# Token-block staging of x, PLE blocks of 272, a w_out block held back and early roots in a hybrid decoder layer

## The chip, the cores and the metric

The kernel runs on the 8 cores of one Trainium2 chip (two dies: cores 0 to 3 and 4 to 7). Each core computes its own share of the batch. The metric is the device time of the slowest core, in microseconds (us). In a slow run one die shows a clearly lower granted TensorE clock than usual. Comparisons use fast runs alone. A median quoted as the time of a kernel is over all its runs, slow ones included; where that matters, the mean of the fast runs is given.

PE is TensorE, PEld its weight loads, DVE is VectorE, ACT is ScalarE, POOL is GpSimd, SP is SyncE.

## The reference, cut to what matters

One layer: a half-step SwiGLU FFN, a mixer (pooling and gated linear attention), one output projection, a second half-step FFN, a gated per-layer embedding (PLE), and a final norm.

```python
h = x + 0.5 * swiglu(rmsnorm(x, ffn1_norm), ...)          # FFN 1, 1024 -> 2816 -> 1024
z = rmsnorm(h, mix_norm) @ w_in                            # mixer: 4 heads
...
mix = sigmoid(ga) * a_out + sigmoid(gb) * (rmsnorm(o) * silu(g))
h = h + mix @ w_out                                        # w_out products
h = h + 0.5 * swiglu(rmsnorm(h, ffn2_norm), ...)           # FFN 2
gate = sigmoid(rmsnorm(h, ple_norm) @ w_ple_gate)          # PLE
h = h + gate * (p @ w_ple_proj)
y = rmsnorm(h, final_norm)
```

A core has 1088 tokens in its first half and 1024 in its last half; it does the whole layer for the first half and then for the last. Values lie feature-major: 128 partitions, 8 groups of features (KC), tokens along the free axis.

## The kernel before

The program is a list of operations that a scheduler (a list scheduler with a cost model) puts in order at build time. Every engine then works through its own list in that order. So an operation that is placed badly holds up those behind it. The parts that the change touches:

```python
FBLK = (tuple((272 * i, 272) for i in range(4)), BLK[1])            # FFN blocks of tokens
PBLK = (BLK[0], ((0, 512), (512, 256), (768, 256)))                 # PLE blocks: 320, 384, 384 in the first half
RESERVE = 3                                                         # PSUM banks kept free for the oldest operation
...
def load_x(self, sb, first):          # x goes straight into the residual h, through hardware queues
    for bi, (st, sz) in enumerate(FBLK[sb]):
        for q in range(0, KC, n):
            self.dma(h[:, q:q + n, st:st + sz], self.xT[sb][:, q:q + n, st:st + sz], ...)
...
# first half, FFN 1: the first weights wait until x has come far enough
self.load_x(sb, first)
self.load_gu(1, 0, after=self.hk(sb, b0[0], b0[1], 1))
self.load_gu(1, 1, after=self.hk(sb, b0[0], b0[1], 7))
prev = []
for bi, (st, sz) in enumerate(FBLK[sb]):
    for k in range(KC):
        self.square(sb, k, st, sz, 'act' if k % 2 == 0 else 'dve', after=prev)
    r = self.norm_rstd(sb, st, sz, 'd')
    prev = K(r)                                        # squares of the next block wait for this root
    self.norm_apply(sb, V_FFN1, st, sz, r)
...
# gate/up: the first 3 of 22 steps are plain products; from step 3 on, 7 products with sums of
# weights (wT, wguh, made by VectorE) and sums of x (sx) replace 8
# mixer, last head: a block's tail, then its own 64 w_out matmuls and the norm of FFN 2
def cur():
    middle(it)
    tail(it)              # ... if hd == 3: w_out of this block
...
# PLE of the first half: all roots and outputs after it, two output buffers
y = [fw.tile("yt%d" % i, [128, 4, W], F32, b1(4 * W * 4)) for i in range(2)]
def finals():
    for bi in range(3):
        root(bi)
    for bi in range(3):
        final(bi)
```

A *root* is the reciprocal square root of a norm on ScalarE: logarithm and exponential, from one table set. The activations of PLE and FFN (tanh, silu) come from another set. A change of set is one table load (1.28 us in these traces).

## Time and profile before

The median is 1588.53 us (runs of 1587.28 to 1588.62 us, one slow one of 1643.35). The profiled run is disturbed on die 1 (granted clock 0.971 to 0.978, against 0.985 on die 0). So stage times of the kernel before are read on cores 0 to 3, and the windows below are of core 0. The spans of die 0 are 1574.9 to 1583.8 us.

From the page of the profile (slowest core): the busy times, then the chain of waits, that is, the work that ended last followed backwards, as shares of the span.

```profile
span 1600.1 us, 29026 instructions; the slowest of 8 cores (1574.9 to 1600.1 us)
...
PE 1503.3 (94%) x9808; PEld 930.3 (58%) x9808; DVE 956.4 (60%) x1898; ACT 758.1 (47%) x1533; POOL 242.4 (15%) x424
...
PE 82%; DVE 7%; DMA 5%; issue 3%; ACT 3%; POOL 0%; DVEq 0%; ACTq 0%; POOLq 0%; SPq 0%
```

PE is the bound. It idles for 1600.1 - 1503.3 = 97 us, and it is mainly these that can be won. Where they lie, the windows view of core 0 says. Its columns: the stretch, its length, the busy time and instructions of each engine, the granted clock (PEclk), the busy share of the DMA engines, and the rate.

```profile
core 0: us, PE busy (x) PEld busy (x) DVE busy (x) ACT busy (x) POOL busy (x), PEclk, DMA share, GB/s
0.00:20.00 20.00, 3.06 (x14) 1.79 (x15) 8.65 (x21) 5.20 (x12) 3.54 (x10) 1.00 0.85 211
20.00:40.00 20.00, 17.98 (x136) 13.28 (x134) 16.00 (x41) 14.13 (x26) 0.00 (x0) 1.00 0.65 134
40.00:60.00 20.00, 18.97 (x161) 15.24 (x159) 14.59 (x40) 7.77 (x20) 4.22 (x8) 1.00 0.71 96
...
510.00:520.00 10.00, 9.54 (x64) 5.74 (x62) 7.38 (x14) 6.37 (x11) 0.00 (x0) 1.00 0.70 182
520.00:530.00 10.00, 10.00 (x69) 6.20 (x67) 4.48 (x9) 4.98 (x10) 0.00 (x0) 1.00 0.26 100
...
870.00:880.00 10.00, 5.56 (x18) 2.04 (x19) 6.29 (x13) 1.79 (x3) 0.53 (x1) 0.66 1.03 252
...
1280.00:1290.00 10.00, 7.53 (x36) 3.28 (x35) 6.03 (x8) 5.39 (x8) 0.00 (x0) 1.00 0.04 13
1290.00:1300.00 10.00, 10.00 (x48) 4.55 (x47) 4.15 (x6) 3.52 (x6) 0.00 (x0) 1.00 0.00 0
1300.00:1310.00 10.00, 4.67 (x21) 1.62 (x18) 4.11 (x7) 5.31 (x7) 0.00 (x0) 1.00 0.00 0
1310.00:1320.00 10.00, 8.79 (x26) 3.10 (x27) 6.96 (x12) 1.12 (x2) 1.14 (x3) 0.66 0.26 38
...
1560.00:1570.00 10.00, 0.38 (x2) 0.13 (x2) 6.09 (x10) 4.18 (x9) 0.00 (x0) 0.69 0.24 90
1570.00:1580.00 10.00, 0.00 (x0) 0.00 (x0) 5.64 (x15) 0.00 (x0) 0.00 (x0) 0.50 0.95 330
```

There are four gaps: the start; 870 us, after the first half's PLE; 1300 to 1320 us, the end of the second mixer; and the last 20 us. At 1310 PE counts as 8.79 of 10 us busy, but it did 26 matmuls where a full stretch has 48: after the idle before, the granted clock was 0.66. The Trainium skill ("TensorE: Matmul & The Clock Gate", "Part 1: The HAM clock gate") says that an idle window of about 3.4 us puts PE's clock to half until it has been busy again. The 0.66 here, a mean over 10 us, agrees with the half: the clock record in the trace has 6.8 us of half clock from 1311.1 us on. But the longest single idle time in the 6.8 us before that was 3.1 us (more in the last section).

What ends the wait at 870 us, from the waits view (engine, line, what it writes, what it waited for: us in total, times, longest), VectorE's line and TensorE's:

```profile
DVE yt L445 <- DMA yT<-yt: 9.5, 2, 6.6
...
PE ps L483 <- DVE snap L450: 7.7, 3, 6.3
```

VectorE waits for a store to leave an output buffer (yt), and PE waits behind VectorE.

### The profile page before, as it was taken

The page shows a single profiled execution, that of the slowest core. Times are in us where ns is not written, and L with a number is a line of the kernel's source. Part 1 is how long each engine was busy: PE and PEld are TensorE (multiplying, and loading weights), DVE is VectorE, ACT ScalarE, POOL GpSimd, SP SyncE. Part 2 cuts the span into 40 slices and gives each one's busy share as a digit, 9 for nine tenths or more (in the row PEclk, how much of TensorE's full clock was granted, in tenths as well). Part 3 has the DMA queues.
Part 4 walks back from the last instruction along what each step waited for, and adds up shares of the span by engine and source line. Part 5 has one row for each costly group of instructions (what it writes and reads, how often), then busy time and mean ns, then how long its engine had stood idle before and what let it go on. Part 6 is the DMA issues. An engine that isn't in the chain of part 4 may idle for free.

```text
span 1600.1 us, 29026 instructions; the slowest of 8 cores (1574.9 to 1600.1 us)
## 1 busy us (share of the span) xinstructions
PE 1503.3 (94%) x9808; PEld 930.3 (58%) x9808; DVE 956.4 (60%) x1898; ACT 758.1 (47%) x1533; POOL 242.4 (15%) x424
## 2 busy tenths in 40 slices
PE   5999999999989999999998899999999988999994
PEld 3788887666656678888753344445555533444444
DVE  6766436677878577743566665236666656664435
ACT  4455314566566456641253344125667543442144
POOL 0221000112100011112061121001021001121113
PEclk9999999999999999999999899999999998999997
DMA  7777642769833355439309875413386004684503
GB/s 173 96 115 122 117 74 47 170 126 185 183 79 80 106 74 86 70 66 151 60 1 209 179 117 100 74 37 49 66 133 99 1 4 73 85 146 80 92 1 106
DMA packets 81633, 153.30 MB, mean 96 GB/s; under 512 B 9520, under 2 KB 23120, under 8 KB 81488
## 3 DMA queue, kind: packets, MB, share of 16 engines
q0 software_dynamic: 53760, 110.22, 43.7%
q1 hardware_dynamic: 27040, 40.64, 8.4%
q8 instruction: 82, 1.34, 0.3%
q10 hardware_dynamic: 688, 0.58, 0.1%
q14 instruction: 63, 0.52, 0.1%
HBM read 243.00 MB, written 18.61 MB: 163 GB/s over the span
## 4 chain that ended last, share of the span: by engine, by line
PE 82%; DVE 7%; DMA 5%; issue 3%; ACT 3%; POOL 0%; DVEq 0%; ACTq 0%; POOLq 0%; SPq 0%
PE ps L483 79%; DVE xn L445 3%; DMA wgu<-w1u 2%; DMA yT<-yt 2%; DVE snap L450 1%; DVE yt L445 1%; ACT nrs L440 1%; DMA wd<-w2d 1%; PE ps L1221 1%; DMA h<-xT 0%; ACT L367 0%; PE ps L1297 0%; PE ps L1299 0%; DMA wgu<-w2u 0%; PE ps L1304 0%
## 5 line engine op out<-in xcount | busy, mean ns | idle before, releaser
L440 ACT ACTIVATE snap<-ps 128x272 f32<-128x272 f32 (+1 forms) x492 | 226.2, 464 | 181.6 <-PE ps L483 163.3
L483 PE MATMUL ps<-xn,wfm 128*128 128x384 bf16 (+2 forms) x1600 | 310.7, 345 | 1.0 <-ACT nrs L440 0.4
L483 PE MATMUL ps<-xn,wgu 128*128 128x272 bf16 (+1 forms) x1488 | 271.8, 319 | 13.5 <-DVE xn L445 12.0
L483 PE MATMUL ps<-hid,wd 128*128 128x272 bf16 (+1 forms) x1892 | 270.3, 305 | 3.1 <-DVE hid L450 2.2
L483 PEld LDWEIGHTS ps<-hid,wd 128*128 128x128 bf16 x1892 | 184.9, 98 | 86.2 <-issue 4.3
L483 PEld LDWEIGHTS ps<-xn,wfm 128*128 128x128 bf16 x1600 | 152.8, 99 | 123.9 <-issue 10.5
L440 ACT ACTIVATE xn<-h 128x272 bf16<-128x272 f32 (+3 forms) x152 | 75.4, 504 | 292.6 <-DVE h L445 284.9
L483 PEld LDWEIGHTS ps<-xn,wgu 128*128 128x128 bf16 x1488 | 146.0, 99 | 100.8 <-issue 34.6
L445 DVE SCALAR_TENSOR_TENSOR h<-ps,h 128x272 f32<-128x272 f32 (+3 forms) x136 | 74.0, 546 | 185.9 <-PE ps L483 185.7
L483 PE MATMUL ps<-sx,wT 128*128 128x272 f16 (+1 forms) x912 | 173.9, 322 | 2.0 <-DVE wT L450 1.4
L450 DVE TENSOR_TENSOR hid<-snap 128x272 bf16<-128x272 f32 (+1 forms) x228 | 118.4, 520 | 65.8 <-ACT snap L440 63.0
L450 DVE TENSOR_TENSOR snap<-ps,snap 128x272 f32<-128x272 f32 (+1 forms) x228 | 114.1, 520 | 44.6 <-PE ps L483 29.5
L483 PEld LDWEIGHTS ps<-sx,wT 128*128 128x128 f16 x912 | 90.8, 100 | 54.9 <-issue 17.3
L483 PE MATMUL ps<-xn,wT 128*128 128x272 bf16 (+1 forms) x456 | 90.1, 321 | 17.8 <-DVE snap L450 17.5
L440 ACT ACTIVATE ps<-ps 128x272 f32<-128x272 f32 (+1 forms) x114 | 51.3, 450 | 114.5 <-PE ps L483 109.7
L445 DVE SCALAR_TENSOR_TENSOR xn<-h,vecs,nrs 128x272 bf16<-128x272 f32 (+3 forms) x168 | 85.2, 581 | 30.2 <-ACT nrs L440 30.1
L367 ACT ACT_TABLE_LOAD x77 | 98.8, 1283 | 4.0 <-issue 2.6
L460 POOL DMA_DIRECT2D wfm<-win_fm x80 | 42.5, 532 | 311.6 <-PE ps L483 131.9
L483 PE MATMUL ps<-xnh,wguh 128*128 128x272 f16 (+1 forms) x456 | 88.2, 317 | 0.1
L483 PE MATMUL ps<-sx,wgu 128*128 128x272 f16 (+1 forms) x456 | 87.9, 316 | 0.0
L460 POOL DMA_DIRECT2D wgu<-w2g x44 | 23.3, 530 | 365.9 <-PE ps L483 311.7
L483 PEld LDWEIGHTS ps<-xn,wT 128*128 128x128 f16 x456 | 43.4, 99 | 48.5 <-issue 31.8
(150 smaller groups left out, 1889.3 us busy)
## 6 DMA issues: line engine op xcount, KB each, us to landing
wfm<-win_fm POOLq DMA_DIRECT2D x80, 256.0 KB, 6.2
wgu<-w1g POOLq DMA_DIRECT2D x44, 256.0 KB, 5.3
wgu<-w1u POOLq DMA_DIRECT2D x44, 256.0 KB, 6.4
wd<-w1d POOLq DMA_DIRECT2D x16, 704.0 KB, 7.0
wgu<-w2g POOLq DMA_DIRECT2D x44, 256.0 KB, 4.2
wgu<-w2u POOLq DMA_DIRECT2D x44, 256.0 KB, 5.2
S0t<-sgla SPq DMA_DIRECT2D x32, 256.0 KB, 6.3
ngs<-S0t SPq DMA_DIRECT2D x32, 256.0 KB, 5.9
```

The lines of the kernel that those rows point to most:

```text
L367: eng.preload_act_table_set(TABLES[tbl])
L440: self.fw.add('act', lambda e: e.activation(out=R(out), in_=R(in_), func=func, **kw), reads, writes, cost=0.19 + n / 1200.0, tbl=tbl)
L445: self.fw.add('dve', lambda e: e.scalar_tensor_tensor(out=R(out), in0=R(in0), scalar=scalar, in1=R(in1), op0=op0, op1=op1), reads, writes, ...
L450: self.fw.add('dve', lambda e: e.tensor_tensor(out=R(out), in0=R(in0), in1=R(in1), op=op), reads, writes, cost=0.16 + n / 960.0)
L460: self.fw.add('pool', lambda e: e.dma_start(out=dst, in_=src), reads=after, writes=[key], dma=sem, cost=nbytes / 330e3)
L483: ins = e.matmul(R(out), lhsT=l, rhs=r, start=(start and i == 0), stop=(stop and i == n - 1), skip_group_check=skip)
L1221: ins = e.matmul(R(pS[:, q * 256:(q + 1) * 256]), lhsT=km[:, q, :], rhs=vS[:, :], start=True, stop=True)
```

## The change

The intent: start PE earlier, and fill or remove the gaps. x and y lie in token blocks in memory. x of the first half is staged in the weights' own queue, interleaved with the first weights, and loaded into h a second time later. PLE of the first half goes in four blocks of 272, with two of the norms and the outputs inside it and four output buffers. In the last head of the mixer, the w_out products of the last but one block are held back beside the last block's tail. Roots are scheduled with priority. The PSUM reservation goes from 3 to 2.

```diff
-PBLK = (BLK[0], ((0, 512), (512, 256), (768, 256)))
+PBLK = (FBLK[0], ((0, 512), (512, 256), (768, 256)))
-    RESERVE = 3
+    RESERVE = 2
@@ scheduler
-                    if best is None or t < best[0]:
-                        best = (t, i, e)
+                    if best is None or t - op['bonus'] < best[0]:
+                        best = (t - op['bonus'], i, e, t)
@@ start of the first half
+        x(0, 4)                 # staging tiles xs, in the weights' queue
+        self.load_gu(1, 0)
+        x(1, 4)
+        self.load_gu(1, 1)
+        x(2, 4)
+        x(3, 4)
+        self.load_gu(1, 2)
...
                 for k in range(KC):
-                    self.square(sb, k, st, sz, 'act' if k % 2 == 0 else 'dve', after=prev)
+                    self.square(sb, k, st, sz, 'act' if (k % 2 == 0 if bi == 0 else k % 4) else 'dve', src=xs)
@@ both halves: x into h from gate/up step 8 on
+        for n, (bi, q) in enumerate((b, q) for b in range(len(FBLK[sb])) for q in (0, 4)):
+            at.setdefault(8 + n, []).append(lambda bi=bi, q=q, n=n: self.load_h(sb, bi, q, 8 + n))
@@ PLE (the roots in both halves, the blocks in the first)
-                self.act(rf[bi][:, 0:sz], ps[:, 0:sz], AF.Copy, [pk], K(rf[bi]))
+                fw.bonus = 2.0
+                self.rsqrt(rf[bi], ps, sz, pk)
+                fw.bonus = 0.0
...
-            for bi in range(3):
+            for bi in range(4):
                 for c in range(KC):
                     ple(bi, c)
+                    if bi < 2:
+                        self.norm_apply(sb, V_PLE, st, sz, rn[bi + 2], ks=(c,))
+                if bi:
+                    final(bi - 1)
-            self.finals = finals
+            self.finals = lambda: final(3)
@@ PLE, last half
-            if c >= 2:
-                ple(0, c - 2)
+            if c >= 4:
+                ple(0, c - 4)
@@ mixer, last head (outp: the w_out products and the norm of a block)
+                if it['hd'] == 3 and it['bi'] < nbk - 2:
+                    outp(it)
...
             else:
-                cur()
+                middle(it)
+                fw.merged([lambda: tail(it), lambda: outp(items[i - 1])])
+                outp(it)
... (cut: layouts of the inputs and outputs, buffers)
```

## The prediction

> **What bounds it now.** TensorE: in the first part of the page PE is busy 1503 of 1600 us (94%), and the chain of waits is 82% PE. So only PE's 97 idle us can be won; the change removes no sizeable matmul. The windows view of the slowest core (7, granted clock 0.974) says where PE idles: 0:60 us 19.8; 60:510 13; 510:570 (end of the first mixer) 7.3; 784:860 (PLE of the first half) 4.9; 860:900 (start of the second half's FFN) 11; 1280:1330 (end of the second mixer) 9.3; 1575:1600 21.
>
> **Step by step.**
>
> 1. Start: gain 1.5 us. Now the first weights are asked for at 11.8, the first weight matmul runs at 20.6, and x's last block arrives at 32.6. In one queue x0, gate/up 0, x1 ... arrive one after the other (Trainium skill, "DMA: Bandwidth & Descriptors", "Queues, rings and completion order": an engine consumes a ring in order, and takes turns between queues). First weight matmul near 12. But the emitted order puts ScalarE's squares of blocks 2 and 3 before the root of block 1, so PE has only block 0 until the last x lands; 4.45 MB of x plus weights at some 300 GB/s (the hardware queue's bytes over its share of busy time) puts that near 26. Ten groups of 16 matmuls (1.84 us each) remain, so the first combined-weight product moves only from 50.3 to 48.5.
>
> 2. x is loaded again into h (4.45 MB while DMA is 75% busy, 100:160). Weights are fetched two steps (17 us) ahead: cost 0.5 us.
>
> 3. End of the mixers: w_out of the previous block (64 matmuls, 10.6 us, second half 13.8) fills the last tail (osq to mix, 9 to 13 us), and the next FFN's first matmuls fill the last norm (now waits of 2.6 and 3.1 us on VectorE's xn). Gain 5 + 7 us.
>
> 4. PLE in four blocks of 272, norms and outputs inside. Now the output products come late, at 843-881, with two yt buffers: VectorE waits 8.8 us for a yT store, and PE behind it 8.3 us (waits view), while reloads of h and weights fill the DMA (share 1.05). Four buffers, early roots and later loads of h remove that. Price: per block about 10 us each of PE, VectorE (8x0.44 + norm 3.3 + output 3.4) and ScalarE (two more table loads of 1.28), so small new stalls. Idle of 784:975 falls from 18 to 8: gain 10 us.
>
> 5. The end: now all roots and outputs wait until 1582, and VectorE works through 24 products until 1595.5. With early roots only eight (3.3 us) remain after the last root: end 4 us of store after 1585. Gain 9.5 us.
>
> Sum 32 us: **1556 us**, 8 in 10 between 1541 and 1571. Faster by over 2%: 0.52, within 2%: 0.46, slower: 0.02.
>
> **What would show it.** PE idle near 65 us with PE busy unchanged; about 10 us after the last matmul, not 20; no PE wait over 4 us near 860-885, none over 2 us at either mixer's end; the first weight matmul near 12, yet the first combined-weight product not before 46.
>
> **What would make it wrong.** x slower than 300 GB/s in the one queue; VectorE, slowed by GpSimd's adds beside it (512-wide xn took up to 1.49 instead of 0.74 us in PLE), or ScalarE's table loads starving PE in PLE; a lower clock on die 1 (0.81-0.93 at 880:950 already); the PSUM reservation going from 3 to 2 reshuffling the steady stages.

## The result, and the profile after

The changed kernel takes 1566.34 us (median of 4 runs: 1562.7, 1563.75 and 1568.93 us, and a slow one of 1645.31). The ratio to the kernel before is 0.9855, 95% interval 0.9821 to 0.989: 1.45% faster, within 2%. The means of the fast runs are 1588.1 us before and 1565.1 us after. Ratios are the mean time of one kernel's fast runs over that of the other's of the same rounds, so not quite the ratio of the medians quoted. The profiled run is fast, with a granted clock of 0.990 to 0.994 on all cores.

```profile
span 1562.2 us, 29356 instructions; the slowest of 8 cores (1552.6 to 1562.2 us)
...
PE 1483.3 (95%) x9896; PEld 933.8 (60%) x9896; DVE 955.6 (61%) x1908; ACT 769.4 (49%) x1559; POOL 253.1 (16%) x440
...
PE 81%; DMA 7%; DVE 5%; issue 3%; ACT 3%; POOL 1%; DVEq 0%; ACTq 0%; POOLq 0%
```

PE's idle time fell from 97 to 1562.2 - 1483.3 = 79 us; 65 had been predicted. PE's busy time fell by 20 us as well. That is not less work: the page before is of a core on the slower die. Between undisturbed cores (the mean of cores 0 to 3 before, of all eight after) idle time fell from 92.9 to 74.7 us and busy time from 1486.4 to 1482.7 us.

Stage by stage, read from the first matmul (or VectorE output) of each stage in the traces. Before is the mean of cores 0 to 3, after the mean of all eight.

| stage | before, us | after, us | change | predicted |
|---|---|---|---|---|
| start to the 9th output of the combined products (the first of gate/up step 5) | 67.2 | 70.7 | +3.5 | -1.5 |
| from there to the first down matmul | 108.9 | 111.3 | +2.4 | +0.5 |
| down | 84.0 | 84.0 | 0 | 0 |
| first mixer, to the next gate/up's first combined product | 313.3 | 312.5 | -0.8 | -5 |
| FFN 2, first half | 207.9 | 209.1 | +1.2 | 0 |
| PLE, first outputs, next gate/up | 198.1 | 190.8 | -7.3 | -10 |
| down | 79.2 | 79.2 | 0 | 0 |
| second mixer, to the next gate/up's first combined product | 264.4 | 251.3 | -13.1 | -7 |
| gate/up, last FFN | 117.1 | 116.5 | -0.6 | 0 |
| last down and PLE, to the last matmul | 119.1 | 124.0 | +4.9 | -9.5 for this row and the next |
| last matmul to the end | 20.3 | 8.0 | -12.3 | |
| sum | 1579.5 | 1557.4 | -22.1 | -32.5 |

The sum of -22.1 us is about what the timed runs show as well (23.0 us between the means of the fast runs). (The terms as written make -32.5; the prediction called it 32.)

The windows of core 0, where before had its gaps:

```profile
core 0: us, PE busy (x) PEld busy (x) DVE busy (x) ACT busy (x) POOL busy (x), PEclk, DMA share, GB/s
0.00:20.00 20.00, 5.00 (x20) 2.29 (x21) 7.95 (x19) 6.30 (x15) 7.78 (x18) 1.00 0.84 184
20.00:40.00 20.00, 15.00 (x104) 11.05 (x103) 10.24 (x25) 14.24 (x28) 0.00 (x0) 0.83 0.49 136
40.00:60.00 20.00, 16.65 (x140) 13.67 (x138) 14.87 (x41) 5.53 (x14) 3.17 (x6) 0.97 0.61 79
...
510.00:520.00 10.00, 7.32 (x52) 4.21 (x52) 6.73 (x14) 4.31 (x8) 0.00 (x0) 1.00 0.82 175
520.00:530.00 10.00, 7.85 (x54) 4.84 (x55) 6.41 (x12) 6.67 (x14) 0.00 (x0) 1.00 0.51 182
...
870.00:880.00 10.00, 10.00 (x48) 4.49 (x46) 6.02 (x13) 4.45 (x8) 1.95 (x4) 1.00 0.59 82
...
1300.00:1310.00 10.00, 10.00 (x48) 4.57 (x47) 8.05 (x13) 1.79 (x3) 2.11 (x4) 1.00 0.44 58
1310.00:1320.00 10.00, 10.00 (x48) 4.50 (x46) 7.38 (x16) 4.15 (x7) 2.11 (x4) 1.00 0.79 114
...
1540.00:1550.00 10.00, 8.96 (x81) 7.61 (x79) 6.59 (x16) 7.39 (x16) 5.16 (x8) 0.99 0.38 154
1550.00:1560.00 10.00, 1.25 (x8) 0.39 (x6) 5.89 (x14) 4.60 (x10) 1.70 (x2) 0.69 0.30 119
```

The gaps at 870 and at 1300 are gone, and the one behind the last matmul is down from 20.3 to 8.0 us. But a new one is at 510 to 530 us, and the start is worse: PE begins earlier (5.00 against 3.06 us before 20 us) and then does 104 matmuls where it did 136.

Why, the timeline of ScalarE on core 0 shows (start, duration, what it does, and the idle time before with what ended it):

```profile
23.52 1.06 ACT L442 ACTIVATE xn<-xs 128x272 bf16<-128x272 f32 x3
25.04 1.07 ACT L442 ACTIVATE xn<-xs 128x272 bf16<-128x272 f32 x3 [0.46 <-DMA xs<-xT]
26.50 1.07 ACT L442 ACTIVATE xn<-xs 128x272 bf16<-128x272 f32 x3 [0.40 <-DMA xs<-xT]
28.83 1.07 ACT L442 ACTIVATE xn<-xs 128x272 bf16<-128x272 f32 x3 [1.26 <-DMA xs<-xT]
29.91 1.28 ACT L369 ACT_TABLE_LOAD   x1
31.21 0.69 ACT L442 ACTIVATE nrs<-ps 128x272 f32<-128x272 f32 x2
```

The squares of blocks 2 and 3 (xn<-xs) stand before the roots of blocks 1 and 2 (nrs<-ps, x2), and three of the four groups wait for their piece of x. So block 1, which had landed at 18.6 us, gets its root at 31.2 us. The blocks were all issued in one queue between 1.6 and 9.1 us and were waited for one after the other until 28.8 us. The Trainium skill ("DMA: Bandwidth & Descriptors", "Queues, rings and completion order") says that each DMA engine consumes the descriptors of a ring in order, which the prediction used; it does not promise that they finish in that order, but here the waits came in the order of issue. And a second time an engine's order costs: the timeline of VectorE a little later, where it makes the weight sums of steps 3 and 4:

```profile
53.22 0.42 DVE L452 TENSOR_TENSOR wT<-wgu,wT 128x512 f16<-128x512 bf16 x1
57.73 0.43 DVE L452 TENSOR_TENSOR wT<-wgu 128x512 f16<-128x512 bf16 x1 [4.10 <-DMA wgu<-w1u]
58.08 0.42 DVE L452 TENSOR_TENSOR wguh<-wgu 128x512 f16<-128x512 bf16 x1
```

The second line is the first sum of step 4, which waits 4.1 us for weights; the third belongs to step 3, whose weights are there (its own first sum ran at 51.25), and stands behind it. PE waits 3.3 us for that wguh.

### The profile page after: what moved, and what is told of

It is laid out like the page before. It is cut to its first block, busy times and chain, and to the rows that moved or that the text cites. A ratio compares the mean times of both kernels' runs of the same rounds, so it can differ in the third digit from the quotient of the medians.

```text
span 1562.2 us, 29356 instructions; the slowest of 8 cores (1552.6 to 1562.2 us)
## 1 busy us (share of the span) xinstructions
PE 1483.3 (95%) x9896; PEld 933.8 (60%) x9896; DVE 955.6 (61%) x1908; ACT 769.4 (49%) x1559; POOL 253.1 (16%) x440
## 4 chain that ended last, share of the span: by engine, by line
PE 81%; DMA 7%; DVE 5%; issue 3%; ACT 3%; POOL 1%; DVEq 0%; ACTq 0%; POOLq 0%
PE ps L485 79%; DMA wgu<-w1u 4%; DMA xs<-xT 1%; DVE snap L452 1%; ACT L369 1%; DMA wgu<-w2u 1%; DVE xn L447 1%; DMA wd<-w2d 1%; POOL h L469 1%; PE ps L1234 1%; DVE yt L447 0%; PE ps L1310 0%; DVE fsg L447 0%; PE ps L1317 0%; ACT nrs L442 0%
## 5 line engine op out<-in xcount | busy, mean ns | idle before, releaser
L485 PE MATMUL ps<-xn,wgu 128*128 128x272 bf16 (+1 forms) x1488 | 266.3, 316 | 7.4 <-DVE xn L447 7.4
L442 ACT ACTIVATE xn<-h 128x272 bf16<-128x272 f32 (+3 forms) x136 | 69.4, 513 | 279.9 <-DVE h L447 279.8
L485 PE MATMUL ps<-sx,wT 128*128 128x272 f16 (+1 forms) x912 | 166.9, 312 | 0.9 <-ACT ps L442 0.9
L369 ACT ACT_TABLE_LOAD x85 | 109.1, 1283 | 2.5 <-PEq L431 1.1
L485 PE MATMUL ps<-xn,wT 128*128 128x272 bf16 (+1 forms) x456 | 86.9, 313 | 12.3 <-DVE snap L452 12.0
L485 PE MATMUL ps<-xn,wpg 128*128 128x272 bf16 (+2 forms) x448 | 66.7, 291 | 9.9 <-ACT fsg L442 9.2
L447 DVE SCALAR_TENSOR_TENSOR xn<-h,vecs,nrs 128x272 bf16<-128x272 f32 (+3 forms) x120 | 65.2, 614 | 16.1 <-ACT nrs L442 15.9
```

The source lines that it names most:

```text
L369: eng.preload_act_table_set(TABLES[tbl])
L442: self.fw.add('act', lambda e: e.activation(out=R(out), in_=R(in_), func=func, **kw), reads, writes, cost=0.19 + n / 1200.0, tbl=tbl)
L447: self.fw.add('dve', lambda e: e.scalar_tensor_tensor(out=R(out), in0=R(in0), scalar=scalar, in1=R(in1), op0=op0, op1=op1), reads, writes, ...
L485: ins = e.matmul(R(out), lhsT=l, rhs=r, start=(start and i == 0), stop=(stop and i == n - 1), skip_group_check=skip)
```

## The experiments

Twelve kernels ran, each with five rounds against the kernel before, all correct. Each group ran on one chip, three chips in all, so times are best compared within a group. The repeated stages give a feeling for the noise of a profile: in the changed kernel and the eight experiments with its start (all but e1, e2, e9, and e5), the way from the start to the first down matmul took 180 to 185 us in means over eight cores; stages in the middle repeat within about 2 us (FFN 2 of the first half, for one, took 208.4 to 210.6 us).

### Group 1: the start, the second load, the reservation, holding back

**e1_oldstart**: the start of the kernel before, no second load of x in the first half.

```diff
-            self.first_loads()
+            self.load_x0()                       # x straight into h, hardware queues
+            self.load_gu(1, 0, after=...)        # as before; squares wait for the previous root
-        for n, (bi, q) in enumerate((b, q) for b in range(len(FBLK[sb])) for q in (0, 4)):
+        for n, (bi, q) in enumerate((b, q) for b in range(len(FBLK[sb])) for q in (0, 4) if not first):
```

> The changed kernel with the start of the kernel before: x goes straight into h through the hardware queues, the first weights wait for x, and x of the first half is not loaded again. Theory A (the start and the second load of x cost about 5 us where the prediction had 1 us of gain): 5 us less than the changed kernel, about 1561; first product with combined weights near 49.7 instead of 52.1 us, and from there to the first down matmul 127 instead of 130 us; all later stages as in the changed kernel. Rival B (those 5 us come from the smaller PSUM reservation or another order of the steady stage, not from the loads): the time stays within 1 us of the changed kernel and that stage stays near 130 us.

Measured: 1559.82 us, ratio 0.9816 (0.9803 to 0.983). In the mean of fast runs this is 8.5 us under e3 below (1558.8 against 1567.3), which is the changed kernel but for one number, on the same chip; by its trace, however, e3 itself is 2.7 us slower than the changed kernel. The first combined product came at 50.8 us (9th output at 66.6, against 70.7) and from there to the first down matmul took 126.5 us. All later stages are within 1 us of the changed kernel's. So theory A holds, and rival B falls: the new start and the second load together cost about 5 us (the first down matmul comes at 177.3 us against 182.0) where the prediction had a gain of 1. Of these, 4.1 us are there by the 9th output, before the second load begins, and 0.6 come after it.

**e2_copy**: the new start; x goes from the staging tiles into h by 32 copies on ScalarE instead of the second load.

```diff
+            for j_, b_ in ((1, 1), (2, 2), (3, 0), (4, 3)):
+                at.setdefault(j_, []).append(lambda b_=b_: self.copy_x(b_))   # ScalarE copies xs into h
-        for n, (bi, q) in enumerate(...):
+        for n, (bi, q) in enumerate(... if not first):
```

> The changed kernel with x of the first half copied into h from its staging tiles by ScalarE (32 copies at the start) instead of a second load of 4.45 MB. Theory A (the second load, which fills the DMA engines at 100 to 160 us, makes the weights late): from the first combined product to the first down matmul 127 us instead of 130, DMA share near 0.8 instead of 1.0 in that stretch; the start itself 0 to 3 us later because ScalarE is busy with copies; total 0 to 3 us less than the changed kernel. Rival B (order or PSUM reservation): that stage stays near 130 us.

Measured: 1568.48 us, ratio 0.988 (0.9867 to 0.9894). From the first combined product to the first down matmul 126.4 us, not 130, with the DMA share on core 0 at 0.81 to 0.89 between 100 and 160 us, in stretches of 20 us, instead of 1.01 to 1.04. But the start got 6 us later (first combined product at 58.1 us), more than the 0 to 3 expected, so nothing was won: ScalarE is the engine that the start cannot spare. The 126.4 flatters, too: with a later start, less of the wait for the weights of steps 3 and 4 falls into it. VectorE's outputs tell the second load's own cost better. From the 25th to the 57th of 76 it takes 52.5 us (means over eight cores) in the kernel before, 56.2 in the changed one and 52.6 here; from there to the last one 34.4, 32.3 and 33.9. So by this comparison the second load costs 3.6 us while it runs, and some 2 us of that are given back in the next 30 us. But e1, which has no second load either, took 54.4 us for the first of these ways (52.8 to 57.3 by core) and 33.6 us for the second. So the load costs 2 to 4 us while it runs, and 0.5 to 2 us in the end. Through which single wait it acts the waits view doesn't say: it lists only small waits of PE for VectorE's snap, 4.1 us in sum on core 0 both with and without the load.

**e3_reserve3**: the PSUM reservation back at 3.

```diff
-    RESERVE = 2
+    RESERVE = 3
```

> The changed kernel with the PSUM reservation of the scheduler back at 3. Theory A: the reservation does next to nothing: within 1.5 us of the changed kernel in the whole, and within 1 us in each gate/up stage. Rival B (the reservation of 2 is what cost the first gate/up stage 3 us, or the mixers): 3 to 5 us faster than the changed kernel, with the stage from the first combined product to the first down matmul at 127 us. Third possibility: the reservation of 2 is part of the gain, then it is slower by some us, at the mixers' ends.

Measured: 1566.88 us, ratio 0.9872 (0.9859 to 0.9886). Gate/up of the first half 128.6 us (130.0), first mixer 317.3 (312.5), the rest within 1 us. Rival B falls: the reservation is not where the gain went. For the third possibility there is the 4.8 us in the first mixer, which the reservation of 2 seems to help, so theory A (next to nothing in the mixers) does not hold cleanly either. Over all stages the traces make e3 2.7 us slower than the changed kernel, and so do the two ratios (0.9872 against 0.9855), but the intervals overlap.

**e4_nohold**: w_out of each block right after its own tail again.

```diff
-                if it['hd'] == 3 and it['bi'] < nbk - 2:
+                if it['hd'] == 3:
                     outp(it)
...
-                middle(it)
-                fw.merged([lambda: tail(it), lambda: outp(items[i - 1])])
-                outp(it)
+                cur()
```

> The changed kernel without the holding back: the w_out products of a block follow its own tail again in both mixers. Theory A (holding back gave about 1 us at the end of the first mixer and all of the 12.8 us of the second): 12 to 14 us slower than the changed kernel, first mixer from start to next gate/up 313 to 314 us instead of 312.5, second 264 instead of 251 us. Rival C (a part of the 12.8 us was the lower granted clock of the profiled run of the kernel before): only 5 to 8 us slower, second mixer near 257 us. Prediction: 12 us slower, 5 in the first mixer and 7 in the second.

Measured: 1577.5 us, ratio 0.994 (0.9928 to 0.9953); 11 us over e3 on the same chip, 16 us over the changed kernel in the second mixer's stage of the trace (267.8 against 251.3 us). The first mixer took 312.5 us, the same as with holding back. Most of the way between 11 and 16 is e3's slower first mixer. The second mixer's stage is also 3.4 us longer than in the kernel before (264.4), so taking the technique out does not quite bring the old program back. So the technique is worth nothing in the first mixer and 13 us (against the kernel before) to 16 us (against e4) in the second, and rival C (the gain came from the clock of one profiled run) falls. The windows of core 0 show what it is made of:

```profile
1280.00:1290.00 10.00, 4.33 (x20) 1.74 (x18) 5.94 (x8) 3.77 (x6) 0.00 (x0) 0.89 0.04 13
1290.00:1300.00 10.00, 10.00 (x37) 4.01 (x36) 2.77 (x4) 1.96 (x4) 0.00 (x0) 0.77 0.00 0
1300.00:1310.00 10.00, 7.83 (x36) 3.21 (x34) 2.77 (x4) 3.48 (x6) 0.00 (x0) 1.00 0.01 2
1310.00:1320.00 10.00, 6.47 (x18) 1.82 (x19) 8.40 (x13) 2.70 (x4) 0.53 (x1) 0.66 0.07 9
```

With 48 matmuls to a full stretch, these 40 us hold 111 of 192, so 81 are missing, 17 us of work. Of the 40 us, 28.6 count as busy: idle time alone accounts for 11.4 us, and the rest of the 17 is slow matmuls at a clock of 0.89, 0.77 and 0.66. In the kernel before, the same 40 us lack 61 matmuls, 12.7 us of work, with 9.0 us of idle time. The prediction counted only the waits: it saw 9.3 us of idle time from 1280 to 1330 us on core 7 and took 7 as the gain. The slow matmuls, 3.7 us, were left out.

### Group 2: order at the start, the tail, the first mixer, the outputs

**e5_rootfirst**: squares of block n+1 wait for the root of block n.

```diff
+            prev = []
-                    self.square(sb, k, st, sz, ..., src=xs)
+                    self.square(sb, k, st, sz, ..., src=xs, after=prev)
                 r = self.norm_rstd(sb, st, sz, 'd')
+                prev = K(r)
```

> The changed kernel, with one more dependency at the start: the squares of block n+1 of x wait for the root of block n, so that ScalarE makes the root of block 1 before it squares blocks 2 and 3. Theory A1 (the start is late because ScalarE, which works in order, holds the root of block 1 behind the squares of blocks that have not landed): weight matmuls of block 1 start near 24 instead of 31 us, first combined product 45 to 48 instead of 52.1, 4 to 7 us less than the changed kernel. Rival A2 (the weights of step 3, which land at 57 us, or x itself bound the start): first combined product stays within 1 us of 52, time the same. The stage after it stays at 130 us under both, as x is still loaded twice.

Measured: 1569.88 us, ratio 0.9864 (0.9848 to 0.988); first combined product at 55.2 us, 3 us later than in the changed kernel. Both theories missed. The root of block 1 did come 6 us earlier (25.1 us) and block 1's weight matmuls began at 27.2 instead of 31.9 us. But the squares of blocks 2 and 3 now run after it, between table loads (the silu of finished products and the roots take turns):

```profile
25.10 0.40 ACT L442 ACTIVATE nrs<-ps 128x272 f32<-128x272 f32 x1
...
26.16 2.03 ACT L442 ACTIVATE xn<-xs 128x272 bf16<-128x272 f32 x6
28.21 1.28 ACT L369 ACT_TABLE_LOAD   x1
```

Block 3's root, without which gate/up step 0 cannot finish and free its weight slot, comes at 40.8 us instead of 36.0, and the weights of step 3 are asked for at 46.8 instead of 44.3 us. So the order that the changed kernel has is not simply wrong. With six of the eight squares of blocks 1 to 3 on ScalarE besides the roots and the silus, ScalarE's serial work, not only its order, looks like what holds the start; the kernel before gives it four of eight squares. That is an inference from this trace, and no run changed the split of the squares alone.

**e6_tail_c2**: PLE of the last half's first block two down steps behind, as before, instead of four.

```diff
-            if c >= 4:
-                ple(0, c - 4)
+            if c >= 2:
+                ple(0, c - 2)
...
-        for c in range(4, KC):
+        for c in range(6, KC):
```

> The changed kernel with PLE of the last half's first block started two down steps behind, as in the kernel before, instead of four. Theory T1 (the 4.9 us that the last stage lost on TensorE come from the early roots: table loads on ScalarE in front of the last blocks' activations): the stretch from the last FFN's first down matmul to the last matmul stays near 124 us (119 in the kernel before). Rival T2 (they come from the shift from two to four steps, which leaves more ScalarE and VectorE work behind the last down product): that stretch falls to 119 to 120 us and the total by 3 to 5 us.

Measured: 1571.43 us, ratio 0.9871 (0.9854 to 0.9889). From the first down matmul to the last matmul 125.4 us, not the 119 to 120 of T2. The shift to four steps is worth 1.4 us in this stage and is not the cause of the loss. T1 stands.

**e7_hold_all**: in the first mixer every block's w_out is held back by one block.

```diff
-                tail(it)
-                if it['hd'] == 3 and it['bi'] < nbk - 2:
-                    outp(it)
+                if it['hd'] == 3 and it['bi'] > 0:
+                    fw.merged([lambda: tail(it), lambda: outp(items[i - 1])])
+                else:
+                    tail(it)
```

> The changed kernel, with each block's w_out products in the first mixer held back by one block: those of block 0 run beside block 1's tail, those of block 1 beside block 2's. Theory M1 (holding back gave nothing in the first mixer because the products that now fill the last tail were taken from the stretch at 510 to 530 us, where they had filled TensorE before): TensorE busy again there (over 9 of 10 us per 10 us instead of 7.3 and 7.9), first mixer from start to the next gate/up 309 to 311 us instead of 312.5, total 2 to 3 us less. Rival M2 (the first mixer's end is bound by VectorE and ScalarE, whatever fills TensorE): no change within 1 us.

Measured: 1568.57 us, ratio 0.9846 (0.9828 to 0.9865), 3 to 4 us under e5, e6 and e8 of the same chip in the mean of fast runs (1566.6 against 1569.4, 1570.8 and 1570.2). First mixer 308.2 us, 4.3 less than in the changed kernel. The windows of core 0 at the place in question:

```profile
510.00:520.00 10.00, 10.00 (x72) 6.48 (x71) 7.25 (x14) 6.73 (x12) 0.00 (x0) 1.00 0.01 2
520.00:530.00 10.00, 9.18 (x64) 5.56 (x62) 6.53 (x14) 4.79 (x11) 0.00 (x0) 1.00 0.66 220
```

PE is busy again (136 matmuls against 106). M1 holds: the change had taken block 1's products from here to fill the last tail, so it moved a gap. The second mixer has two blocks only, and there the stretches from 1230 to 1270 us are fully busy in the changed kernel. Only the next 10 us lost a little (8.14 us busy against 8.87 in the kernel before), so hardly anything was taken from a place that needed it.

**e8_lateout**: the first half's roots and outputs all after its PLE, as before the change; four blocks and four buffers stay.

```diff
-                fw.bonus = 2.0
-                self.rsqrt(rf[bi], ps, sz, pk)
+                self.act(rf[bi][:, 0:sz], ps[:, 0:sz], AF.Copy, [pk], K(rf[bi]))   # first half only
...
-                if bi:
-                    final(bi - 1)
-            self.finals = lambda: final(3)
+            self.finals = finals                  # 4 roots, then 4 outputs
```

> The changed kernel with the first half's roots and output products all after its PLE, as before the change, but with the four blocks of 272 and four output buffers kept. Theory P1 (early outputs made the gain of 9.5 us in the stretch from the first half's PLE to the next FFN's first down matmul): that stretch goes from 191 back to 197 to 201 us and the total grows by 6 to 10 us. Rival P2 (the four buffers, or x loaded into h later, made it; the early output is not needed): within 2 us of the changed kernel.

Measured: 1570.02 us, ratio 0.9869 (0.985 to 0.9888); PLE to the next down matmul 192.9 us (190.8). P1 falls, early outputs are worth 2 us of it. (The 9.5 us in the expectation took the kernel before over all eight cores, 200.4 us; on its undisturbed die it is 198.1, so 7.3.)

### Group 3: the best of both, the outputs again, the roots

**e9_best**: e1 and e7 together (edits as there).

> The changed kernel with two things that earlier runs showed to be better: the start of the kernel before (x straight into h, no second load in the first half) and the w_out products of every block of the first mixer held back by one block. If the two gains (4.7 us and 4.3 us in the stages of the traces) are independent: 8 to 10 us less than the changed kernel, about 1557 us at the clock of the first timings, ratio to the kernel before 0.979 to 0.981; first combined product near 50 us, first mixer from start to the next gate/up 308 to 309 us. If they collide (the mixer's weights come at another time): only 5 to 6 us.

Measured: 1562.75 us, ratio 0.9816 (0.9801 to 0.9831). First combined product at 51.5 us, first mixer 309.5. Its last matmul ends at 1545.7 us in the mean over cores, against 1553.6 in e10 of the same chip, where start and mixer are as in the changed kernel; the means of the fast runs are 1562.4 and 1569.4. So the gains add up to about 7 us, a little under the 8 to 10 expected. Against the kernel before this is 1.8% instead of 1.45%. It was not run side by side with the changed kernel or with e1 (whose ratio is the same 0.9816), so that it beats e1 is not shown.

**e10_hnow**: x of the last half into h at once after the outputs, as before the change.

```diff
             self.finals()
+            for bi in range(2):
+                for q in (0, 4):
+                    self.dma(self.h[:, q:q + 4, st:st + sz], self.xsrc(sb, bi, q), ...)
```

> The changed kernel, but x of the last half is loaded into h at once after the first half's last outputs, as in the kernel before, instead of from gate/up step 8 on. Rival P2b (the later load of h made the 9.5 us in the stretch from the first half's PLE to the next FFN's first down matmul, because it no longer fills the DMA engines while weights and outputs are moved): that stretch grows from 191 to 196 to 200 us. P2a (the four output buffers made them): it stays at 191 to 192 us. The load of h may only start when the outputs have been made, so a part of P2b may be hidden: 193 to 195 us would say both.

Measured: 1572.47 us, ratio 0.986 (0.984 to 0.988); stage 191.5 us. P2b alone falls.

**e11_late2**: late outputs (as e8) and only two output buffers.

```diff
-            yt = {(bi, q): y[2 * (bi % 2) + q] for bi in range(4) for q in range(2)}
+            yt = {(bi, q): y[q] for bi in range(4) for q in range(2)}
```

> The changed kernel with the late outputs of the last set and, besides, only two output buffers as in the kernel before; the four blocks of 272 and the late load of h stay. P2a (four buffers made the gain): VectorE waits for stores to leave the buffers, TensorE waits behind it some 6 to 8 us on VectorE, stretch from PLE to the next FFN's first down matmul 197 to 200 us, against 193 with late outputs and four buffers. P2b (the later load of h made it): stays at 193 to 194 us, as the stores now find free DMA engines.

Measured: 1573.51 us, ratio 0.9882 (0.9865 to 0.9898); stage 192.5 us, and VectorE's waits on core 0 list no wait for a store at all. P2a falls too. What remains is told below.

**e12_noprio**: no priority for the roots in the last half.

```diff
-                fw.bonus = 2.0
+                fw.bonus = 0.0 if last else 2.0
```

> The changed kernel without the priority for the roots in the last half: the scheduler then puts all three roots behind the last activation of PLE, with one table load, and all outputs after them. Theory T1 (early roots cost TensorE 4 to 5 us by table loads in ScalarE's queue, and save more than that after the last matmul): from the last FFN's first down matmul to the last matmul 120 to 121 us instead of 124, but 19 to 21 us from there to the end instead of 8: 7 to 10 us slower in all. Rival T3 (the roots do not matter; the shorter end comes from the token-block layout of the outputs): end still 8 to 10 us after the last matmul, time 2 to 4 us less than the changed kernel.

Measured: 1570.5 us, ratio 0.9866 (0.985 to 0.9883). To the last matmul 117.5 us (124.0 with priority), and from there to the end 17.5 us (8.0). T1 holds and T3 falls: the priority costs PE 6.5 us and saves 9.5 us behind it, 3 us net, less than the 7 to 10 expected. The times show no more than a hint of that (ratios of 0.9866 and 0.9855, intervals that overlap). How it costs PE, the changed kernel's ScalarE on core 0 shows:

```profile
1531.10 1.28 ACT L369 ACT_TABLE_LOAD   x1
1532.40 0.60 ACT L442 ACTIVATE rf<-ps 128x512 f32<-128x512 f32 x1
...
1533.62 0.70 ACT L442 ACTIVATE sqf<-h 128x256 bf16<-128x256 f32 x2
1534.35 1.28 ACT L369 ACT_TABLE_LOAD   x1
1535.64 0.94 ACT L442 ACTIVATE fsg<-ps 128x256 f32<-128x256 f32 x3
```

and its TensorE behind that:

```profile
1533.75 0.38 PE L485 MATMUL ps<-pb,wpp 128*128 128x256 bf16 x2
1536.17 1.37 PE L485 MATMUL ps<-xn,wpg 128*128 128x256 bf16 x8 [2.04 <-ACT fsg L442]
...
1538.19 1.92 PE L485 MATMUL ps<-xn,wpg 128*128 128x256 bf16 x8
...
1540.23 1.04 PE L485 MATMUL ps<-xn,wpg 128*128 128x256 bf16 x8
```

Between two tanh (fsg<-ps) lie two table loads, a root and squares, about 5 us. PE waits 2.04 us for a tanh, and its next groups of eight matmuls take 1.37 and 1.92 us instead of 1.04, at a granted clock of 0.84 in this stretch of 10 us.

## Why the prediction was right or wrong

The time of 1566.34 us lies in the range of 1541 to 1571, and the class "within 2%" had a chance of 0.46. But the central value was 10 us too low and the likelier class was the other one. By its terms:

1. **Start: the step that failed.** Predicted -1.5, measured +3.5 us at the end of step 4. The order of ScalarE (squares of blocks 2 and 3 before the root of block 1) was seen rightly, and so was the work left behind it (ten groups of 16 matmuls predicted, 164 matmuls in the trace). Three sizes were missed, read on core 0. The last x was waited for until 28.8 us, not 26, so the rest began at 31.9 us. It took 20.4 us, not 18.4: PE had just waited 2.2 and 2.8 us for squares, and the trace has half clock from 28.0 to 34.9 us, which costs 1.5 us of matmuls. And VectorE's order made PE wait 3.3 us for a weight sum behind the first combined products. "First weight matmul near 12" was 16.1 in the mean of the cores. e1 shows that the old start is better; e5 that one more dependency does not mend the new one.

2. **Second load of x.** Predicted +0.5; the stage shows +2.4, and the two experiments without the load (e1, e2) put its own cost at 2 to 4 us while it runs and 0.5 to 2 us net. So asking for the weights two steps ahead did not hide the load while it ran; through which wait it acts stays open.

3. **Ends of the mixers.** Predicted -5 and -7, measured -0.8 and -13.1. The mechanism was right where there are two blocks. The size was off, since idle time was counted but not the lower clock that follows it (kernel before: 61 missing matmuls, 12.7 us, with 9.0 us of idle time; e4: 81, 17 us, with 11.4). In the first mixer the term failed: the products moved came from a place that needed them (e7, which holds back every block, takes 308.2 us there, 4.3 under the changed kernel and the predicted 5 under the kernel before).

4. **PLE and first outputs.** Predicted -10, measured -7.3. The wait for stores is gone, as predicted. Its cause is only half settled. Late outputs cost 2 us (e8), early loads of h nothing (e10), two buffers nothing on top of late outputs (e11). So no one of the three makes the gain: either each is enough to keep the stores from colliding with the loads (in the kernel before the DMA share was 1.03 at 870 to 880 us, with all three against it), or the blocks of 272 with the norms inside made it. The run with all three undone at once, which would tell the two apart, was not made. A third rival stands beside them: the layout of y in token blocks, which every experiment kept. From 820 to 900 us on core 0 (the DMA view of the profile, medians) the stores took 8.4 and 15.8 us from issue to landing in the kernel before (640 and 768 KB) and 2.9 us in e11 (544 KB), though both have late outputs and two buffers; with h loaded early (e10) they took 3.7 us.

5. **The end.** Predicted -9.5, measured -7.4 (-12.3 behind the last matmul, +4.9 before it). The prediction had "about 10 us after the last matmul", and 8.0 came. It named table loads as a danger and set no cost for them. e12 puts 6.5 us on the roots' priority, and e6 shows that the other shift of the tail (two to four steps) has no part in that.

The rest, FFN 2 of the first half at +1.2 us and the last gate/up at -0.6, is about the noise of these stages. The sum of misses: 5.0 + 1.9 + 4.2 - 6.1 + 2.7 + 2.1 + 0.6 = 10.4 us, which is -22.1 against -32.5. That it is no more than this is partly luck: the other terms together fell 16.5 us short, and the second mixer's 6.1 us, mis-sized the other way, made up for a part. Of the rivals named beforehand, the reservation (e3) and the granted clock of one run (e4) are not the cause.

## What to carry to other kernels

Work that is moved to fill a gap comes from somewhere: look at the place it leaves before you count the gain, as in the first mixer. A gap on TensorE costs its idle time and then slow matmuls, so count the missing matmuls of a stretch rather than the waits. And a root put early on an engine that works through its list in order is paid for by what stands behind it, here with two changes of the function table: TensorE lost 6.5 us for the 9.5 that were saved.

## What the Trainium skill lacked or had wrong

- "ScalarE: Activation LUTs", "What ACT_TABLE_LOAD costs", gives about 1283 ns for the load and about 1380 ns of drain, 2.66 us for a switch. The load is right (mean of 85 in the changed kernel: 1283 ns). No drain shows: a load at 1531.10 lasts 1.28 us and the next activation starts at 1532.40, and the loads start within 0.01 to 0.02 us of the activation before them.
- "TensorE: Matmul & The Clock Gate", "Part 1: The HAM clock gate", speaks of an idle window of about 3.4 us before the clock falls. Here shorter waits were enough: in the tail, after one wait of 2.04 us, the trace has 3.4 us of half clock (a group of eight matmuls took 1.92 instead of 1.04 us). The clock record of core 0 has seven stretches of half clock in each of the two kernels, all but the last 3.4 us long or twice that, and in the 6.8 us before each of them no single idle time was longer than 3.35 us. That part of the page doesn't say how little work in a window counts as idle.
- The same page, "Seeing it yourself", says that once three cores of a die run dense matmuls the die's clock goes to 13/16 for as long as the load lasts, and to budget for that. Here eight cores at 95% PE busy held 0.990 to 0.994 in the changed kernel's profiled run, whose clock record has no 13/16 at all. Only some runs showed such a state, mostly on one die: in one of e1's, cores 4 to 7 were at 0.811 to 0.818 (13/16 is 0.8125) and took 1813 to 1824 us, while cores 0 to 3 took 1547 to 1556 us. Nor did it always hold: in the profile of the kernel before, the cores of die 1 have 18 or 22 stretches at 13/16, of 3.7 to 7.9 us each, and those of die 0 none. No page says that it comes in some executions of a kernel and not in others.
